# A hybrid decoder trunk: first loads in halves, another order of pairs in the in-projection, and two up-projection weights kept in place

## The chip, the cores and the metric

The kernel runs on one core of a Trainium2 chip. The metric is device time in microseconds (us) of one execution. The engines are TensorE (PE: matmuls; PEld: its weight loads), VectorE (DVE), ScalarE (ACT), GpSimd (POOL) and SyncE (SP). SP, POOL and, since this change, ACT issue DMA transfers; an issue waits in its engine's queue behind whatever stands ahead of it.

## The reference

One layer of a decoder trunk, batch 1, 1,024 positions, model width 1,024, all in float32:

```python
h = rms_norm(x, g_mix)
z = einsum("bsd,de->bse", h, w_in) + b_in          # 1024 -> 7168 columns
va, ga, xb, gb, sa, sb = split(z)                  # 1024, 1024, 1536, 1536, 1024, 1024
u = va * sigmoid(ga)
u = silu(layer_norm(causal_depthwise_conv(u, width 31)))
y_a = u @ w_a_out
v = rg_lru(causal_depthwise_conv(xb, width 4), ...)  # block-diagonal gates, linear recurrence
y_b = (v * gelu(gb)) @ w_b_out
m = sigmoid(sa) * y_a + sigmoid(sb) * y_b
x = x + m @ w_o
h = rms_norm(x, g_mlp)
x = x + square(relu(h @ w_1)) @ w_2                 # 1024 -> 4096 -> 1024
return rms_norm(x, g_final)
```

## The kernel before

**Precision.** Every float32 operand of a matmul is split into a high part, a copy rounded to the matmul's format, and a low part, the difference. Each product is three matmuls: high by high, high by low, low by high. `split` makes the low part on DVE. `split_dma` makes it by a transfer: ACT writes the negated rounded copy, a POOL DMA adds the source to it in place (256 or 512 KB), and ACT writes the high part.

**The start.** x comes twice: transposed, in tiles `xc` (two column blocks of 128 channels by 512 positions each), and in rows (`xt`), from which the squares for the RMS norm are taken. Three weight blocks, `w0` to `w2`, are loaded beside it. SP issues these loads in a fixed order: `gmix` (the norm's gain), `w0`, four `xc` tiles of the first half of the positions (half 0), `w1`, `w2`, four row tiles, the other `xc` tiles, the other row tiles. While the first data are under way, PE runs matmuls on ones (`idle_mm`). Then, with the instruction order of PE, ACT and DVE written out by hand: for each channel block `c`, ACT makes the scaled high part (`x_plain`), DVE the low part (`x_plain_low`), and PE runs `first_z`. The first half of the positions is multiplied without the row scale 1/rms. The second half needs it: `x_square` squares and sums four row tiles, `x_root(1)` makes the reciprocal root on DVE with one ACT step, `x_spread(1)` spreads it on PE into the tile `rb`, in the middle of `first_z(2, ...)`. Small DVE steps for the recurrence's decay constants (`decay`, run some at a time by `decay_on`) fill DVE's free time.

**The in-projection.** The first part goes block by block of 128 output columns (`chunk_mm`) and makes all the recurrent columns (XB) and most convolution columns (VA, GA). The second part (lines 743 and on) takes the remaining columns in pairs of blocks with seven products instead of eight (Winograd's form of Strassen's scheme). `ZPAIRS` lists the pairs: six of the Gelu gate GB, one of VA with GA, four of SA, four of SB. `zseq` interleaves the seven products of neighbouring pairs:

```python
for i in range(2, NZ):
    zseq += [(i, 1), (i, 7), (i - 1, 4), (i, 6), (i, 2), (i - 1, 3), (i, 5)]
```

In step n of `zseq` the kernel evacuates step n - 1 or n - 2 (`z_post`, `z_post2`), multiplies (`z_mm`), splits the weights for step n + 4 (`z_lhs`, of which five in seven use `split_dma`) and makes the sums for step n + 5 (`z_sums`). A pair's four outputs come out after its products 2, 5, 3 and 4. `z_out` applies Gelu to GB columns, multiplies them by the recurrence's result `h`, which SP loads some steps ahead (`z_h`), and stores the product; it applies a sigmoid to SA and SB columns and stores that. DVE also works through the 31 taps of the wide convolution here, where it has time. `ZL` gives the steps at which a pair's raw weights are loaded.

**Up-projection.** The MLP's up part is again a seven-product scheme on 16 pairs of blocks of `w_1`. `raws[i, m]` holds the raw weights of pair i, half m (512 KB each). The products 1 and 2 of the first four pairs are made early, at the end of the list `gseq`, from `raws[i, 0]` (`g_lhs` with "u"). For pairs 2 and 3 `g_lhs` drops `raws[i, 0]` after product 2. Later, in the loop over `useq`, both halves of a pair that isn't there are loaded:

```python
up_load(i, [m_ for m_ in (0, 1) if (i, m_) not in raws])
```

`GX[u0 + n]` lists extra work that is issued with step n of the early products. SP's queue there holds the row tiles of x1 that are written out (`x1d`), the loads, and the stores of the early products' results (`fd`). The split weights of this part (`gu`, `o`) get their low parts by `split_dma`.

Of the kernel before, what the change touches and what calls it, by code (L numbers as in the profile page):

```python
# [9 lines left out]
F32 = mybir.dt.float32  # L10
F32R = mybir.dt.float32r
I32 = mybir.dt.int32
AF = mybir.ActivationFunctionType
ALU = mybir.AluOpType

P = 128
# [14 lines left out]
def trunk_kernel(ctx: ExitStack, tc: tile.TileContext, x, xt_in, xt_eo, vecs, w_in, w_a_out, w_b_pl, w_b_sq,  # L31
                 w_rg, w_o, w_1, w_2, g_final, out):

    nc = tc.nc
# [9 lines left out]
    def T(name, dt=F32, shape=(P, S)):  # L44
        return tp.tile(list(shape), dt, tag="T", name=name)

    def PS(name, tag="ps"):
        return pp.tile([P, S], F32, tag=tag, name=name, bufs=1 if tag == "ps2" else 3)
# [5 lines left out]
    HALVES = (slice(0, HS), slice(HS, S))  # L54


    def load_w(w, name):

        raw = wp.tile(list(w.shape), F32, tag="raw", name=name + "_raw")
        nc.sync.dma_start(raw, w)  # L60
        return raw
# [56 lines left out]
    wp = stage.enter_context(tc.tile_pool(name="weights", bufs=2))  # L118
# [8 lines left out]
    vec = cp.tile([P, 448], F32, name="vec")  # L127

    gmix = cp.tile([P, 16], F32, name="gmix")
    nc.sync.dma_start(gmix[:, 0:8], vecs[:, 0:8])  # L130
    nc.gpsimd.dma_start(vec, vecs)
    gmix_c = gmix[:, 0:8]
    bin_c = vec[:, 8:64]
# [11 lines left out]
    xt, xc, raw0 = [], [], []  # L145
# [6 lines left out]
    def load_xc(hf, c2):  # L152
        a = T(f"xc{hf}{c2}")
        nc.sync.dma_start(a, xt_in[hf, c2])
        xc.append(a)

    def load_w0(i):
        if i < 2:
            raw0.append(load_w(w_in[(16, 0, 8)[i]], f"w{i}"))
        else:  # L160
            raw0.append(T(f"w{i}_raw").rearrange("p (k c) -> p k c", c=P))
            nc.sync.dma_start(raw0[i], w_in[(16, 0, 8)[i]])

    load_w0(0)
    for c2 in range(4):
        load_xc(0, c2)
    load_w0(1)
    load_w0(2)
# [12 lines left out]
    def xpart(a, hf, c):  # L181
        return a[hf][c // 2][:, HALVES[c % 2]]

    rs_x = {}

    def x_square(t, eng):

        hf, i = divmod(t, 4)
        if hf not in rs_x:
            rs_x[hf] = cp.tile([P, 5, 4], F32, tag="st4", name=f"stx{hf}", bufs=2)  # L190
        a, ss = xt[(t + 4) % 8], rs_x[hf][:, 0, i:i + 1]
        if eng is nc.vector:
            nc.vector.scalar_tensor_tensor(a, a, 1.0, a, ALU.mult, ALU.mult, accum_out=ss)
        else:
            nc.scalar.activation(a, a, AF.Square, accum_out=ss)
# [28 lines left out]
    def x_plain(c):  # L224

        u = xc[c // 2][:, HALVES[c % 2]]
        nc.scalar.activation(xpart(xh, 0, c), u, AF.Copy, scale=gmix_c[:, c:c + 1])

    def x_plain_low(c):
        u, h = xc[c // 2][:, HALVES[c % 2]], xpart(xh, 0, c)  # L230
        nc.vector.scalar_tensor_tensor(xpart(xl, 0, c), u, gmix_c[:, c:c + 1], h.bitcast(F32),
                                       ALU.mult, ALU.subtract)
# [8 lines left out]
    w0 = []  # L241

    def first_w(i, part):
        if part == "h":
            if i < 2:
                wh = wp.tile([P, 8, P], F32R, tag="wh", name=f"w{i}_h")
                wl = wp.tile([P, 8, P], F32R, tag="wl", name=f"w{i}_l")
            else:
                wh, wl = (T(f"w{i}_{n}", F32R).rearrange("p (k c) -> p k c", c=P) for n in "hl")
            w0.append((wh, wl))  # L250
            z0.append(PS(f"z{16 + i}"))
            nc.scalar.activation(wh, raw0[i], AF.Copy)
        else:
            nc.vector.tensor_tensor(w0[i][1], raw0[i], w0[i][0].bitcast(F32), ALU.subtract)

    def first_z(i, hf, k, which):
        w, a = {"hh": (0, xh), "lh": (1, xh), "hl": (0, xl)}[which]
# [72 lines left out]
    def decay_on(n=99):  # L330

        for _ in range(n):
            next(decaying, None)

    with tc.manual_schedule(engines={mybir.EngineType.Activation, mybir.EngineType.DVE,
                                     mybir.EngineType.PE}):
        warm = cp.tile([P, 10], F32, name="warm")
        nc.vector.memset(warm[:, 0:2], 1.0)
        nc.scalar.activation(warm[:, 0:1], warm[:, 1:2], AF.Sqrt)

        spare = PS("spare", "ps2")

        def idle_mm(n):
            for _ in range(n):
                nc.tensor.matmul(spare[:, 0:P], ones, ones, start=True, stop=True)

        idle_mm(13)
        rb["tile"] = PS("rb", "ps2")
        first_w(0, "h")
        first_w(0, "l")  # L350
        for c in range(8):
            x_plain(c)
            x_plain_low(c)
            if c == 7:
                first_w(1, "h")
                first_w(1, "l")
            for which in ("hh", "lh", "hl"):
                first_z(0, 0, c, which)
        for k in range(8):
            first_z(1, 0, k, "hh")  # L360
            first_z(1, 0, k, "hl")
        decay_on(6)
        first_w(2, "h")
        first_w(2, "l")
        decay_on(14)
        for t in range(4, 8):
            x_square(t, nc.scalar)
        for k in range(8):
            first_z(1, 0, k, "lh")
        x_root(1)  # L370
        decay_on(5)
        for k in range(8):
            first_z(2, 0, k, "hh")
            first_z(2, 0, k, "hl")
            if k == 4:
                x_spread(1)
        for k in range(8):
            first_z(2, 0, k, "lh")

        for c in range(9):  # L380
            if c < 8:
                x_scaled(1, c)
            else:
                x_root(0)
                x_spread(0)
            if 3 <= c < 7:
                x_square(c - 3, nc.scalar)
            if c:
                for which in ("hh", "lh"):
                    first_z(0, 1, c - 1, which)  # L390
                x_low(1, c - 1)
                first_z(0, 1, c - 1, "hl")
                for i in range(1, N0):
                    first_z(i, 1, c - 1, "hh")
                    first_z(i, 1, c - 1, "hl")
        for i in range(1, N0):
            for k in range(8):
                first_z(i, 1, k, "lh")
        decay()
        nc.vector.tensor_scalar(cab2, cab_c, 2.0, None, ALU.mult)  # L400
        pairs = caw[:, 8:].rearrange("p (i o j) -> p i o j", o=2, j=8)
        nc.vector.tensor_tensor(csum, pairs[:, :, 0, :], pairs[:, :, 1, :], ALU.add)
# [24 lines left out]
    VA, GA, XB, GB, SA, SB = 0, 8, 16, 28, 40, 48  # L427
# [267 lines left out]
    def later(ready, cost, f, *a):  # L695

        todo.append((ready, len(todo), cost, f, a))
# [28 lines left out]
                                 start=n == 0, stop=n == 23)  # L726
        at("P", len(halves) * (n1 - n0) * MM)

    ZPAIRS = [GB + 2 * i for i in range(6)] + [VA + 7] + [SA + 2 * i for i in range(4)]
    ZPAIRS += [SB + 2 * i for i in range(4)]  # L730
    NZ = len(ZPAIRS)
    zraw, zs, zo, zb = {}, {}, {}, {}
    zn = [0]

    def z_load(i, kk):

        zraw[i, kk] = raw = qp.tile([P, 2, 4, P], F32, tag="p", name=f"zw{i}_{kk}", bufs=4)
        c = ZPAIRS[i]
        if c < GA:
# [47 lines left out]
    for i in range(2, NZ):  # L787
        n = zseq.index((i, 1))
# [20 lines left out]
    with tc.manual_schedule(engines=ENGINES):  # L809
        for s in range(3, NC1):  # L810
# [30 lines left out]
            c = CH[s - 1]  # L841
# [27 lines left out]
            for d in range(5):  # L869
                if s - d in EXP:  # L870
# [6 lines left out]
                    t = 3 * g + d - (2 if g < 3 else 1)  # L877
# [21 lines left out]
    wp = stage.enter_context(tc.tile_pool(name="weights2", bufs=3, reuse_waits="tile"))  # L899
# [59 lines left out]
    def z_out(i, m_, hf, src, name):  # L959
        if ZPAIRS[i] < GA:  # L960
            z_u(i, ZPAIRS[i] - VA, m_, hf, src)
            return
        ci = ZPAIRS[i] + m_
        bias = bin_c[:, ci:ci + 1]
# [58 lines left out]
    with tc.manual_schedule(engines=ENGINES):  # L1023
# [159 lines left out]
        for n in range(len(zseq) + 2):  # L1183
# [9 lines left out]
            if n + 3 < len(zseq):  # L1193
                i, p = zseq[n + 3]
# [15 lines left out]
    wp = early.enter_context(tc.tile_pool(name="weights3", bufs=7, reuse_waits="tile"))  # L1210
# [191 lines left out]
    def g_lhs(w, i, p):  # L1402
        if w == "u":
            src = raws[i, 0][:, 4 * (p - 1):4 * p, :]
            if p == 2 and i > 1:
                del raws[i, 0]
        elif p in (5, 6):
            src = gs[w, i][p - 5 and 1]
        else:
            src = graw[w, i, {1: 0, 2: 1, 3: 1, 7: 0, 4: 1}[p]][:, int(p == 4)]  # L1410
        go[w, i, p] = o = T(f"g{w}{i}_{p}", F32R).rearrange("p (x k c) -> p x k c", x=2, c=P)
        if w == "a" and p in (1, 2, 7):
            nc.scalar.activation(o[:, 0], src, AF.Copy)
            later(at("A", 0.6), 0.63, low, o[:, 1], src, o[:, 0])
        else:
            split_dma(src, o[:, 0], o[:, 1])
            at("A", 1.15)
# [238 lines left out]
    raws = {}  # L1656
# [113 lines left out]
    def g_get(n, f):  # L1770
# [32 lines left out]
        0: ((up_lhs, 0, 6), (x1_rows, 4, 5, 6, 7)),  # L1803
        1: ((x1_diag, 1),), 2: ((x1_spread, 1), (up_lhs, 1, 6)),
        3: ((x1_normed, 0, 1), (x1_normed, 1, 1), (g_t, "u", 0, 1), (g_t, "u", 1, 1)),
        4: ((g_t, "u", 0, 2), (g_t, "u", 1, 2)), 5: ((g_parts, "u", 6, 0),),
        6: ((g_parts, "u", 6, 1), (g_parts, "u", 5, 0), (up_lhs, 0, 5)),
        7: ((g_parts, "u", 5, 1), (up_lhs, 1, 5), (g_t, "u", 0, 3), (g_t, "u", 1, 3))}.items()})
    BX = {}
# [147 lines left out]
    with tc.manual_schedule(engines={mybir.EngineType.Activation, mybir.EngineType.DVE,  # L1957
                                     mybir.EngineType.PE}):
        for n in range(len(useq)):
# [4 lines left out]
            while ready < min(len(useq), n + look + 1):  # L1964
                i, p = useq[ready]
# [167 lines left out]
    with tc.manual_schedule(engines={mybir.EngineType.Activation, mybir.EngineType.DVE,  # L2133
                                     mybir.EngineType.PE}):
        for n, (g, p, kk) in enumerate(dseq[:-2]):
# [41 lines left out]
            if (g, m - 4) in XADD:  # L2177
                k = XADD[g, m - 4]
# [103 lines left out]
```

## Time and profile before

| | |
|---|---|
| Median of 3 runs | 1531.3 us (1531.1 to 1531.85) |
| Profiled execution, device time | 1531.15 us |
| Its span, first to last instruction | 1529.4 us |
| Granted PE clock | 0.999 of full speed |
| First matmul on real data | 7.17 us |
| Second part of the in-projection | about 339 to 626 us |
| Early products of the up part | about 907 to 933 us |
| Last instruction's stage: time after the last matmul | some 7 us |

Times in the profile count from the start of the span. A busy share is that of a stretch. An engine's idle time is put down to what ended it; several semaphores to the one that came last.

### The profile page before, as it was taken

How to read it: one execution, taken by the hardware profiler on the slowest of the kernel's cores; microseconds unless marked ns; L12 is line 12 of the kernel's file. 1: busy time of each engine (PE TensorE's matmuls, PEld its weight loads, DVE VectorE, ACT ScalarE, POOL GpSimd, SP SyncE). 2: the span in 40 equal slices, each digit the busy share in tenths (PEclk: the TensorE clock that was granted, in tenths of full speed). 3: DMA queues.
4: the chain of work that ended last, by engine and by line, in shares of the span. 5: the costliest groups of instructions: out<-in, count | busy, mean ns of one | idle time of the engine just before them, and what ended most of it. 6: DMA issues, size and time to landing. Idle time of an engine off the chain costs nothing.

```text
span 1529.4 us, 18963 instructions
## 1 busy us (share of the span) xinstructions
PE 1519.5 (99%) x6722; PEld 1251.2 (82%) x6722; DVE 1200.0 (78%) x1636; ACT 928.3 (61%) x1299; POOL 192.3 (13%) x228
## 2 busy tenths in 40 slices
PE   9999999999999999999999999999999999999998
PEld 7878887888888888888888887888888888888886
DVE  6899996998999997788869879755555387777777
ACT  6748688576566667645575777554444455545475
POOL 0111011022222222000022332000000000101010
PEclk9999999999999999999999999999999999999999
DMA  9766779797997889964879897333333974776465
GB/s 352 188 146 154 184 159 204 196 258 209 265 261 173 186 207 271 297 226 119 269 201 302 188 205 195 138 122 111 111 111 111 302 265 131 177 211 169 107 123 153
DMA packets 130799, 296.53 MB, mean 194 GB/s; under 512 B 12896, under 2 KB 34912, under 8 KB 130704
## 3 DMA queue, kind: packets, MB, share of 16 engines
q1 hardware_dynamic: 98960, 215.92, 42.0%
q0 software_dynamic: 31600, 79.15, 28.1%
q8 instruction: 52, 0.85, 0.2%
q14 instruction: 43, 0.35, 0.1%
q10 hardware_dynamic: 144, 0.26, 0.0%
HBM read 149.79 MB, written 60.82 MB: 138 GB/s over the span
## 4 chain that ended last, share of the span: by engine, by line
PE 96%; issue 2%; DVE 1%; POOL 1%; DMA 0%; ACT 0%; POOLq 0%; ACTq 0%
PE z L725 16%; PE z L258 2%; PE d1b L2002 2%; PE d2b L2002 2%; PE d0b L2002 2%; PE d3b L2002 2%; PE d0e L2002 1%; PE d3e L2002 1%; PE d3a L2002 1%; PE d2e L2002 1%; PE d2a L2002 1%; PE d1e L2002 1%; PE d1a L2002 1%; PE d0a L2002 1%; PE rg L532 1%
## 5 line engine op out<-in xcount | busy, mean ns | idle before, releaser
L725 PE MATMUL z<-xh,win_h 128*128 128x512 f32 x368 | 115.4, 391 | 0.0
L725 PE MATMUL z<-xl,win_h 128*128 128x512 f32 x368 | 114.9, 390 | 0.0
L637 DVE SCALAR_TENSOR_TENSOR y<-u,vec,y 128x511 f32<-128x511 f32 (+14 forms) x120 | 88.2, 735 | 0.0
L725 PE MATMUL z<-xh,win_l 128*128 128x512 f32 x368 | 87.4, 389 | 0.0
L637 DVE SCALAR_TENSOR_TENSOR yt<-u,vec,yt 128x511 f32<-128x511 f32 (+6 forms) x112 | 82.5, 736 | 0.0
L637 DVE SCALAR_TENSOR_TENSOR y<-yt,csum,y 128x511 f32<-128x511 f32 (+6 forms) x112 | 82.4, 736 | 0.0
L725 PEld LDWEIGHTS z<-xh,win_h 128*128 128x128 f32 x368 | 69.1, 188 | 16.0 <-ACT win_h L67 0.5
L725 PEld LDWEIGHTS z<-xl,win_h 128*128 128x128 f32 x368 | 69.1, 188 | 14.9
L725 PEld LDWEIGHTS z<-xh,win_l 128*128 128x128 f32 x368 | 69.1, 188 | 14.6
L542 ACT ACTIVATE g<-rg,vec 96x1024 f32<-96x1024 f32 x32 | 35.5, 1110 | 72.9 <-PE rg L534 72.8
L1697 ACT ACTIVATE o<-s 128x512 fp32r<-128x512 f32 x56 | 33.7, 623 | 45.7 <-DVE s L1681 26.4
L66 POOL DMA_DIRECT2D zo<-zw x45 | 39.2, 871 | 133.8 <-ACT zo L65 110.4
L483 DVE SCALAR_TENSOR_TENSOR v<-xb,vec,v 128x1023 f32<-128x1023 f32 (+2 forms) x36 | 46.2, 1282 | 6.3 <-ACT v L474 5.3
L66 POOL DMA_DIRECT2D db_10l<-br x4 | 3.5, 877 | 339.6 <-DMA br<-in_w_dram 254.4
L66 POOL DMA_DIRECT2D win_l<-win_raw x23 | 20.0, 868 | 194.0 <-ACT win_l L65 155.9
L65 ACT ACTIVATE zo<-zw 128x512 fp32r<-128x512 f32 x45 | 28.2, 626 | 24.3 <-PE z10f L929 2.1
L1219 DVE TENSOR_TENSOR o<-s,o 128x512 fp32r<-128x512 f32 x56 | 37.2, 683 | 1.3 <-ACT o L1697 1.3
L66 POOL DMA_DIRECT2D zo<-zs x30 | 26.4, 879 | 75.9 <-ACT zo L65 63.8
L67 ACT ACTIVATE zo<-zw 128x512 fp32r<-128x512 f32 x45 | 27.9, 621 | 0.0
L578 DVE TENSOR_TENSOR_SCAN g<-a,g 128x1024 f32<-128x1024 f32 x12 | 27.5, 2291 | 0.4
L66 POOL DMA_DIRECT2D ga<-gsa x8 | 7.0, 874 | 161.0 <-DMA m<-mbd 150.8
L1219 DVE TENSOR_TENSOR o<-w_raw,o 128x512 fp32r<-128x512 f32 x38 | 25.9, 683 | 0.0
(3182 smaller groups left out, 4912.0 us busy)
## 6 DMA issues: line engine op xcount, KB each, us to landing
w_raw<-in_w_dram SPq DMA_DIRECT2D x34, 512.0 KB, 5.7
br<-in_w_dram SPq DMA_DIRECT2D x32, 512.0 KB, 6.1
ar<-fd SPq DMA_DIRECT2D x32, 512.0 KB, 7.0
zw<-in_w_in_dram SPq DMA_DIRECT2D x28, 512.0 KB, 6.9
win_raw<-in_w_in_dram SPq DMA_DIRECT2D x23, 512.0 KB, 5.0
win_l<-win_raw POOLq DMA_DIRECT2D x23, 512.0 KB, 5.2
zo<-zw POOLq DMA_DIRECT2D x45, 256.0 KB, 5.7
gates<-zg SPq DMA_DIRECT2D x32, 256.0 KB, 4.1
```

Source lines behind the costliest of these rows:

```text
L65: nc.scalar.activation(l, src, AF.Copy, scale=-1.0)
L66: nc.gpsimd.dma_start(l, src, accum_op=ALU.add)
L67: nc.scalar.activation(h, src, AF.Copy)
L258: nc.tensor.matmul(z0[i][:, HALVES[hf]], w0[i][w][:, k, :], xpart(a, hf, k), start=k == 0 and which == "hh", stop=k == 7 and which == ("hl ...
L483: nc.vector.scalar_tensor_tensor(v[:, d:S], a[:, 0:S - d], cbw_c[:, w * 12 + t:w * 12 + t + 1], v[:, d:S], ALU.mult, ALU.add)
L542: nc.scalar.activation(a, gps.pop((n, gi))[:HD, :], AF.Sigmoid, bias=(ba_c, bx_c)[gi][:, n:n + 1])
L578: nc.vector.tensor_tensor_scan(i, a, i, 0.0, ALU.mult, ALU.add)
L637: nc.vector.scalar_tensor_tensor(o[:, k:], a[:, 0:HS - k], c, o[:, k:], ALU.mult, add)
L725: nc.tensor.matmul(zps[s][:, HALVES[hf]], w[:, k, :], xw[k][part][hf], start=n == 0, stop=n == 23)
L1219: tt(l, src, h.bitcast(F32), ALU.subtract)
L1697: nc.scalar.activation(o[:, 0], src, AF.Copy)
L2002: nc.tensor.matmul(o, a, b, start=start and n == 0, stop=stop and n == len(todo) - 1, skip_group_check=not start or not stop)
```

## The change

1. At the start, `w0` and the first `xc` tile are loaded in halves, on two queues: SP takes the first half of `w0`, `gmix`, and the second half of `xc`; ACT the first half of `xc` and the second half of `w0`. `w0` is split in halves too (`first_half`), the second after channel block 2. Nine `idle_mm` instead of thirteen (each is a pair of passes in the profile).
2. Of the four squares of the row tiles 4 to 7 one (t == 6) is made by DVE, and the four stand ahead of `decay_on(14)` instead of behind it.
3. `ZPAIRS` alternates GB pairs with SA pairs; VA + 7 and the four SB pairs keep their places.
4. `raws[2, 0]` and `raws[3, 0]` are kept, and the other halves of these pairs are loaded at step u0 + 4.

```diff
-    nc.sync.dma_start(gmix[:, 0:8], vecs[:, 0:8])
     nc.gpsimd.dma_start(vec, vecs)
...
-    load_w0(0)
-    for c2 in range(4):
+    raw0.append(wp.tile([P, 8, P], F32, tag="raw", name="w0_raw"))
+    xc.append(T("xc00"))
+    nc.sync.dma_start(raw0[0][:, 0:4], w_in[16, :, 0:4])
+    nc.scalar.dma_start(xc[0][:, HALVES[0]], xt_in[0, 0, :, HALVES[0]])
+    nc.sync.dma_start(gmix[:, 0:8], vecs[:, 0:8])
+    nc.scalar.dma_start(raw0[0][:, 4:8], w_in[16, :, 4:8])
+    nc.sync.dma_start(xc[0][:, HALVES[1]], xt_in[0, 0, :, HALVES[1]])
+    for c2 in range(1, 4):
         load_xc(0, c2)
...
-            nc.scalar.activation(wh, raw0[i], AF.Copy)
+            if i:
+                nc.scalar.activation(wh, raw0[i], AF.Copy)
...
+    def first_half(n):
+        k = slice(4 * n, 4 * n + 4)
+        h, l = (a[:, k] for a in w0[0])
+        nc.scalar.activation(h, raw0[0][:, k], AF.Copy)
+        nc.vector.tensor_tensor(l, raw0[0][:, k], h.bitcast(F32), ALU.subtract)
...
-        idle_mm(13)
+        idle_mm(9)
         rb["tile"] = PS("rb", "ps2")
         first_w(0, "h")
-        first_w(0, "l")
+        first_half(0)
         for c in range(8):
             x_plain(c)
             x_plain_low(c)
+            if c == 2:
+                first_half(1)
...
         first_w(2, "h")
         first_w(2, "l")
+        for t in range(4, 8):
+            x_square(t, t == 6)
         decay_on(14)
-        for t in range(4, 8):
-            x_square(t, nc.scalar)
...
-    ZPAIRS = [GB + 2 * i for i in range(6)] + [VA + 7] + [SA + 2 * i for i in range(4)]
-    ZPAIRS += [SB + 2 * i for i in range(4)]
+    ZPAIRS = [GB, GB + 2, SA, GB + 4, SA + 2, GB + 6, VA + 7, SA + 4, GB + 8, SA + 6, GB + 10] + [SB + 2 * i for i in range(4)]
...
             src = raws[i, 0][:, 4 * (p - 1):4 * p, :]
-            if p == 2 and i > 1:
-                del raws[i, 0]
...
-        4: ((g_t, "u", 0, 2), (g_t, "u", 1, 2)), 5: ((g_parts, "u", 6, 0),),
+        4: ((up_load, 2, (1,)), (up_load, 3, (1,)), (g_t, "u", 0, 2), (g_t, "u", 1, 2)), 5: ((g_parts, "u", 6, 0),),
```

More of the change, by code (lines that the diff above doesn't have):

```diff
@@ L184, in trunk_kernel, with x_square @@
     rs_x = {}
-    def x_square(t, eng):
+    def x_square(t, dve=False):
         hf, i = divmod(t, 4)
@@ L191, in x_square @@
         a, ss = xt[(t + 4) % 8], rs_x[hf][:, 0, i:i + 1]
-        if eng is nc.vector:
+        if dve:
             nc.vector.scalar_tensor_tensor(a, a, 1.0, a, ALU.mult, ALU.mult, accum_out=ss)
@@ L386, in trunk_kernel @@
             if 3 <= c < 7:
-                x_square(c - 3, nc.scalar)
+                x_square(c - 3)
             if c:
```

## The prediction

> **What bounds the kernel now.** I read the page's engine table and chain first, then busy time by stretches, then TensorE's (PE) waits, and last the timelines of the three places that the change touches.
>
> ```profile
> span 1529.4 us, 18963 instructions
> PE 1519.5 (99%) x6722; PEld 1251.2 (82%) x6722; DVE 1200.0 (78%) x1636; ACT 928.3 (61%) x1299; POOL 192.3 (13%) x228
> PE 96%; issue 2%; DVE 1%; POOL 1%; DMA 0%; ACT 0%; POOLq 0%; ACTq 0%
> ```
> ```profile
> 340.00:538.00 198.00, 198.00 (x875) 163.99 (x874) 183.88 (x285) 127.64 (x218) 46.47 (x53) 1.00 0.86 217
> 373.00:563.00 190.00, 190.00 (x840) 157.35 (x839) 177.59 (x278) 120.54 (x208) 47.35 (x54) 1.00 0.88 221
> 933.00:945.00 12.00, 11.67 (x52) 9.34 (x50) 10.93 (x12) 11.82 (x20) 5.25 (x6) 1.00 0.82 189
> ```
> ```profile
> PE f0d L1709 <- DMA o<-s: 0.8, 1, 0.8
> ```
>
> PE is busy 99% of the span and carries 96% of the chain. In the in-projection's second part (340 to 538 us) it has no idle time at all: a new order of pairs can win nothing there, it can only lose. After the start, PE's list of waits has one entry, 0.8 us for an `o<-s` transfer in the stretch 933 to 945. So the change has two places to win in: the start, and that wait. No multiplication is added or removed.
>
> **The start.** The timeline there, by engine:
>
> ```profile
> 0.74 0.39 SPq L130 DMA_DIRECT2D gmix<-in_vecs_dram  x1
> 1.18 0.42 SPq L60 DMA_DIRECT2D w_raw<-in_w_in_dram  x1
> 1.60 5.92 PE L345 MATMUL spare<-ones 128*128 128x128 f32 x26 [1.60 <-POOL ones L113]
> 4.95 1.06 ACT L252 ACTIVATE w_h<-w_raw 128x1024 fp32r<-128x1024 f32 x1 [2.72 <-DMA w_raw<-in_w_in_dram]
> 7.17 0.70 PE L258 MATMUL z<-xh,w_h 128*128 128x512 f32 x1
> 14.51 1.06 ACT L195 ACTIVATE x<-x 128x1024 f32<-128x1024 f32 x1 [0.21 <-DMA x<-in_x_dram]
> 17.09 1.06 ACT L195 ACTIVATE x<-x 128x1024 f32<-128x1024 f32 x1 [0.15 <-DMA x<-in_x_dram]
> 18.36 1.06 ACT L195 ACTIVATE x<-x 128x1024 f32<-128x1024 f32 x1
> 16.31 0.17 DVE L286 SCALAR_TENSOR_TENSOR sm<-sm 128x12 f32<-128x12 f32 x1
> 18.80 0.17 DVE L293 TENSOR_TENSOR sm<-sm 128x12 f32<-128x12 f32 x1
> 19.54 0.17 DVE L202 TENSOR_SCALAR stx<-stx 128x4 f32<-128x4 f32 x1 [0.58 <-ACT x L195]
> 21.50 1.13 PE L217 MATMUL rb<-rd,ones 128*128 128x128 f32 x8
> ```
> ```profile
> L483 DVE SCALAR_TENSOR_TENSOR v<-xb,vec,v 128x1023 f32<-128x1023 f32 (+2 forms) x36 | 46.2, 1282 | 6.3 <-ACT v L474 5.3
> ```
>
> The loads are one stream. ACT's squares at 14.51 and 17.09 each wait for a 512 KB tile that has just landed: two tiles in 2.58 us, 1.29 each. Halves change the order within the stream, not its rate. They move its beginning: the first weight was issued at 1.18 behind gmix, and the half now goes at 0.74, so 0.44 earlier. From 1.18 to the landing that starts ACT at 4.95 are 3.77 us for one tile, 2.48 over the steady 1.29; a second issuing queue could win back part of that ramp. I bound the stream's shift by 0 (2 KB pieces may be slower) and 1.4, and take 0.5, close to the row of the issue. ACT's two issues, by SP's rows 0.39 to 0.42 each, end long before its first data.
>
> PE may begin earlier: nine pairs of warming matmuls instead of thirteen take 4 x 5.92/13 = 1.8 us less, and halves split after half a tile. That is cover only as long as nothing later holds PE back. One thing does: PE must have the row scale `rb` in the middle of the third column block. In the trace it comes at 21.50, right behind PE's arrival, and its chain is the fourth x tile: square at 18.36, `x_root` on VectorE (DVE) at 19.54, `rb` 1.96 later.
>
> Here the change moves work onto that chain. The square of the third tile (t == 6) goes to DVE, and the fourteen decay steps, which ran from 16.31 to 18.97 beside the wait, now stand behind it in DVE's queue and ahead of `x_root`. The tile lands at 17.09 - 0.5 = 16.6. No trace row shows a DVE square with a sum; the nearest, 1,023 elements of the same operation, takes 1.28 (below: ACT's 1.06; above: half as much again for the sum). So 16.6 + 1.28 + 2.66 + 1.96 = 22.5 for `rb` against 21.50. ACT's chain, a square shorter, is done earlier and no longer counts. PE waits, and everything behind it shifts: **+1.0**. With the stream's bounds +0.1 to +1.5. What PE won before 21 us is lost in this wait.
>
> **The order of pairs.** Gate pairs (GB, Gelu) and sigmoid pairs (SA, VA) now alternate. Loads, sums, splits and matmuls per pair are the same; what changes is which function ACT needs next. From the timeline of ACT at the one such border in the trace, with the transfer that follows it:
>
> ```profile
> 462.14 1.28 ACT L944 ACT_TABLE_LOAD   x1
> 463.44 0.69 ACT L944 ACTIVATE u<-z6a,vec 128x512 f32<-128x512 f32 x1
> 464.02 0.62 ACT L65 ACTIVATE zo<-zw 128x512 fp32r<-128x512 f32 x1
> 465.18 1.28 ACT L969 ACT_TABLE_LOAD   x1
> 467.06 0.62 ACT L65 ACTIVATE zo<-zs 128x512 fp32r<-128x512 f32 x1
> 480.57 1.28 ACT L980 ACT_TABLE_LOAD   x1
> ```
> ```profile
> 467.98 0.87 POOL L66 DMA_DIRECT2D zo<-zs  x1 [2.16 <-ACT zo L65]
> ```
> ```profile
> DMA to landing us min/median/max: 7.4/7.4/7.4
> DMA to landing us min/median/max: 4.2/6.7/9.3
> ```
> ```profile
> 476.19 2.72 PE z7b L929 x12
> ```
>
> Two neighbouring pairs interleave their outputs (old, new, old, new), so a border of unlike functions costs three table loads: 462.14, 465.18, 480.57. Before there was one border inside the list; now there are nine (1|2, 2|3, 3|4, 4|5, 5|6, 7|8, 8|9, 9|10, 10|11): 8 x 3 = 24 more loads of 1.30 us (462.14 to 463.44), 31 us of ACT. ACT is busy 120.5 of the 190 us from 373 to 563, so 31 fit into its 69 idle us on the whole.
>
> Locally less so. Two loads fall into neighbouring steps, ahead of ACT's `zo` splits, whose low half a DMA then finishes. The split at 467.06 is one of those delayed; its DMA was issued at 467.98 and landed after 7.4 us, at 475.4. The step that uses it, z7b, stands at 476.19 and needs it with its third matmul, 0.45 later: 1.2 to spare. With the slowest landing of this stretch (first number pair: this one DMA; second: all of 373 to 545), 9.3 instead of 7.4, PE would wait 0.7. Of the 32 splits under the eight new borders I take two that meet such a landing: **+1.4**; ends 0 (as at the border shown) and +5.6 (one at every border).
>
> The Trainium skill, page "ScalarE: Activation LUTs", section "What ACT_TABLE_LOAD costs", puts a switch to another set at about 2.66 us, load and drain together, and its rules ask to do all of one set before switching. The row does not bear out the drain (the next activation starts 1.30 after the load); by the page's price the 24 would be 64 us, nearly all of ACT's idle time here.
>
> **Up weights kept.** Two reloads of 512 KB (the first halves of pairs 2 and 3) go; the two loads that remain are issued at the fifth step of the up part instead of behind the fourth store of `f`. The pieces of timeline, POOL, SP and PE:
>
> ```profile
> 917.24 0.95 POOL L66 DMA_DIRECT2D gu<-w_raw  x1 [5.90 <-ACT gu L65]
> 937.92 0.87 POOL L66 DMA_DIRECT2D o<-s  x1 [0.65 <-ACT o L65]
> 912.63 4.68 SPq L1585 DMA_DIRECT2D x1d<-x1r  x4
> 938.81 6.63 SPq L1664 DMA_DIRECT2D w_raw<-in_w_dram  x3
> 925.32 0.72 PE L1427 MATMUL gu1a<-gu2h,gu 128*128 128x512 f32 x2
> 945.45 0.73 PE L1709 MATMUL f0d<-gu7h,o 128*128 128x512 f32 x2 [0.77 <-DMA o<-s]
> ```
> ```profile
> DMA to landing us min/median/max: 8.0/8.0/8.0
> ```
>
> The `o<-s` of 937.92, for which PE waits until 945.45, shares the engines with the three `w_raw` loads that SP issues from 938.81. With those gone it lands before its step: -0.8, and some 0.2 of slow matmuls beside it. But from 912.63 SP writes four 512 KB rows out, and `gu<-w_raw` of 917.24 needed 8.0 us (the row above) and landed at 925.25, just when PE uses it (925.32). The two kept loads now queue on SP right behind those rows: 2 x 1.29 = 2.6 us of transfers where there is no slack. They may find no free buffer so early and come later; then SP's four stores of `f` stand behind them, which nobody reads before the down-projection. Ends -1.0 and +1.6; I take half a microsecond lost of the gain: **-0.5**.
>
> **Sum.** +1.0 + 1.4 - 0.5 = +1.9. The profiled execution took 1531.15 (span 1529.4 and 1.75 around it), 0.15 under the median of the runs, 1531.3. So 1533.0. A measurement of this kernel tells about 0.2%, 3.06 us, from no change: under 1528.2 is faster, over 1534.4 slower.
>
> **Rivals.**
> *The start wins.* If the stream comes 1.4 earlier and the DVE chain is not what ends last, `rb` can't come more than the stream's 1.4 earlier than now; with the whole -1.0 of the up weights and no cost in the pairs that is 1528.7, with the 0.5 of the issue row 1529.6. Against it: the decay steps' place in DVE's queue. Chance 0.17.
> *ACT late among the alternating pairs.* A pair's seven steps take 7 x 2.72 = 19.0 us, of which ACT works 19 x 120.5/190 = 12.1; three loads make 16.0. It decides once the lead of the splits is used up: about 1.2 us at a border, as worked out above, so from landings of 8.6 us on, or from a switch that holds ACT for more than (19.0 - 12.1)/3 = 2.3 us. The first, at four of five borders, is 0.7 x 6 = 4.2 over the start's +1.0 and the -0.5: 1535.9. The second would be (12.1 + 3 x 2.66 - 19.0) x 8 = 8.6 us, but the row's 1.30 speaks against it. Chance 0.23. The page named above stands with the second: by its price ACT falls behind in every pair; that part I give 0.03.
> *The kept loads collide.* +1.6 in place of -0.5: 1535.1. For it: the landing without slack at 925; against: buffers may come free later. Chance 0.10.
> The forecast keeps 0.50.
>
> **Numbers.** The forecast's own cases lie between 1531 and 1534.3. The range 1530.0 to 1535.8 leaves out the best start (about 0.08) and the worst ACT cases (about 0.1). Slower by over 0.2%: most of the second and third rivals and a little of the forecast, 0.28. Faster by over 0.2% needs the stream's full bound and every other gain: 0.05. The rest, 0.67, is no change.
>
> **What would show it.** Right: the first `z` matmul near 5.7 us, yet a PE wait of about a microsecond before `rb`, with DVE's decay steps between the t == 6 square and `x_root`; 28 table loads in place of 4 between 340 and 626 us, ACT some 31 us busier, and a few PE waits under 1 us for `zo` transfers; no wait at f0d, perhaps one at gu1a. Wrong: `rb` before 21.3; no PE wait at all among the pairs, or many; a gain or loss of PE elsewhere than in these three places.

## The result, and the profile after

The kernel after takes 1535.05 us (median of 9 runs, 1533.4 to 1536.41), the one before 1531.11 beside it (9 runs, 1530.6 to 1531.85): a ratio of 1.0026, with a 95% interval of 1.0017 to 1.0035. It is slower by 0.26%, 3.9 us, just above the 0.2% from which the prediction calls a difference a change. The profiled execution took 1535.94, 0.9 above the median, with a span of 1534.2, 4.8 us more than the 1529.4 of before; the terms read from it below are together that 0.9 above those of the median. The page of the profile after, span, engines and chain:

```profile
span 1534.2 us, 18973 instructions
PE 1520.0 (99%) x6714; PEld 1249.4 (81%) x6714; DVE 1202.0 (78%) x1639; ACT 956.8 (62%) x1322; POOL 192.2 (13%) x228
PE 93%; DMA 3%; DVE 1%; issue 1%; ACT 0%; POOL 0%; SPq 0%; POOLq 0%; DVEq 0%; ACTq 0%
```

PE has as much work as before (1520.0 us busy against 1519.5), ACT 28.5 us more, and DMA has 3% of the chain where it had none. PE's waits after (engine, tile and line, what it waited for: us in total, times, longest):

```profile
PE spare L357 <- POOL ones L113: 1.6, 1, 1.6
PE z L270 <- ACT xh L232: 1.3, 1, 1.3
PE z4e L942 <- DMA zo<-zs: 1.2, 1, 1.2
PE gu1a L1438 <- DMA gu<-w_raw: 1.1, 1, 1.1
PE rb L222 <- DVE rd L213: 0.8, 1, 0.8
PE z7f L942 <- DMA zo<-zw: 0.5, 1, 0.5
PE z L270 <- DVE xl L236: 0.2, 1, 0.2
```

The wait at f0d is gone. Each of the three places has new ones: at the start (`z` twice, `rb`), two among the pairs (`z4e`, `z7f`), one in the up part (`gu1a`). PE waits nowhere else, but for the first warming matmul, as before.

**The start.** The timeline after; the rows of before stand in the prediction:

```profile
5.82 0.52 PE L270 MATMUL z<-xh,w_h 128*128 128x512 f32 x1
9.36 0.50 PE L270 MATMUL z<-xh,w_h 128*128 128x512 f32 x1 [1.31 <-ACT xh L232]
17.54 1.23 DVE L198 SCALAR_TENSOR_TENSOR x<-x 128x1024 f32<-128x1024 f32 x1 [0.28 <-DMA x<-in_x_dram]
18.69 0.17 DVE L298 SCALAR_TENSOR_TENSOR sm<-sm 128x12 f32<-128x12 f32 x1
21.27 0.16 DVE L207 TENSOR_SCALAR stx<-stx 128x4 f32<-128x4 f32 x1
18.82 1.06 ACT L200 ACTIVATE x<-x 128x1024 f32<-128x1024 f32 x1 [1.41 <-DMA x<-in_x_dram]
21.47 0.20 ACT L97 ACTIVATE stx<-stx 128x4 f32<-128x4 f32 x1 [1.50 <-DVE stx L207]
23.22 1.13 PE L222 MATMUL rb<-rd,ones 128*128 128x128 f32 x8 [0.79 <-DVE rd L213]
```

PE begins 1.35 us earlier (5.82 against 7.17) and is at `rb` 1.72 later (23.22 against 21.50). From 17.54 to 21.27 DVE does the third tile's square and then the fourteen decay steps, while ACT, done with the fourth tile, waits 1.50 us for DVE's first step of `x_root`. And the row tiles come later than before, not earlier: the fourth starts ACT at 18.82 instead of 18.36.

**The pairs.** The groups of ACT's table loads between 340 and 630 us after, the stretch 373 to 563 by engine, and the timeline ahead of the wait at z4e:

```profile
L982 ACT ACT_TABLE_LOAD x14 | 18.0, 1283 | 2.8 <-PE z5a L942 0.5 <-PE z10a L942 0.5 <-PE z8a L942 0.5
L993 ACT ACT_TABLE_LOAD x13 | 16.7, 1283 | 0.2
L957 ACT ACT_TABLE_LOAD x1 | 1.3, 1283 | 0.0
```
```profile
373.00:563.00 190.00, 188.32 (x829) 155.32 (x829) 175.94 (x275) 145.11 (x226) 46.31 (x53) 1.00 0.87 218
```
```profile
427.12 1.28 ACT L993 ACT_TABLE_LOAD   x1
430.16 1.28 ACT L982 ACT_TABLE_LOAD   x1
435.21 1.28 ACT L993 ACT_TABLE_LOAD   x1
437.18 0.62 ACT L65 ACTIVATE zo<-zs 128x512 fp32r<-128x512 f32 x1
438.39 0.87 POOL L66 DMA_DIRECT2D zo<-zs  x1 [1.98 <-ACT zo L67]
446.96 0.72 PE L942 MATMUL z4e<-xh,zo 128*128 128x512 f32 x2 [1.21 <-DMA zo<-zs]
```

28 loads, and idle time of PE where it had none: 1.68 us. Three table loads stand in the 10 us ahead of the split at 437.18; its transfer, issued at 438.39, landed after 8.5 us, and PE had been waiting for it since 445.75.

**The up part.** The timeline after:

```profile
916.62 4.63 SPq L1596 DMA_DIRECT2D x1d<-x1r  x4
921.43 2.71 SPq L1675 DMA_DIRECT2D w_raw<-in_w_dram  x2
921.24 0.95 POOL L66 DMA_DIRECT2D gu<-w_raw  x1 [5.90 <-ACT gu L65]
930.50 0.74 PE L1438 MATMUL gu1a<-gu2h,gu 128*128 128x512 f32 x2 [1.10 <-DMA gu<-w_raw]
```

SP issues the two kept pairs' loads right behind the four rows of x1, within 0.2 us of the `gu` transfer of which PE has no slack. That lands after 9.2 us (8.0 before), and PE waits.

By the trace that is +1.72 at the start, +2.2 among the pairs (two waits, with the slow matmul behind each) and +0.87 in the up part (+2.1 at gu1a to gu3a, less 0.2 that was lost there before and 1.05 at f0d): together the 4.8 of the span.

### The profile page after: what moved, and what is told of

Same layout as the page of the kernel before. It is cut to its first block, busy times and chain, and to the rows that moved or that the text cites. A ratio compares the mean times of both kernels' runs of the same rounds, so it can differ in the third digit from the quotient of the medians.

```text
span 1534.2 us, 18973 instructions
## 1 busy us (share of the span) xinstructions
PE 1520.0 (99%) x6714; PEld 1249.4 (81%) x6714; DVE 1202.0 (78%) x1639; ACT 956.8 (62%) x1322; POOL 192.2 (13%) x228
## 4 chain that ended last, share of the span: by engine, by line
PE 93%; DMA 3%; DVE 1%; issue 1%; ACT 0%; POOL 0%; SPq 0%; POOLq 0%; DVEq 0%; ACTq 0%
PE z L739 16%; PE d1b L2013 2%; PE d2b L2013 2%; PE d0b L2013 2%; PE d3b L2013 2%; PE d0e L2013 1%; PE d3e L2013 1%; PE d3a L2013 1%; PE d2e L2013 1%; PE d2a L2013 1%; PE d1e L2013 1%; PE d1a L2013 1%; PE d0a L2013 1%; PE z L270 1%; PE rg L546 1%
## 5 line engine op out<-in xcount | busy, mean ns | idle before, releaser
L497 DVE SCALAR_TENSOR_TENSOR v<-xb,vec,v 128x1023 f32<-128x1023 f32 (+2 forms) x36 | 46.2, 1283 | 5.8 <-ACT v L488 4.8
```

Source lines behind the costliest of these rows:

```text
L497: nc.vector.scalar_tensor_tensor(v[:, d:S], a[:, 0:S - d], cbw_c[:, w * 12 + t:w * 12 + t + 1], v[:, d:S], ALU.mult, ALU.add)
```

## The experiments

Twelve kernels, each in 11 runs beside runs of the kernel before on the same chip. What lies around the span scatters from 1.7 to 3.7 us, so the median of the spans is shown too; it is the sharper of the two. By the time alone, e1 (only just) to e3 are slower and e10 to e12 faster than the kernel before; the intervals of e4 to e9 include no change, and what is said of these rests on their spans and traces.

| run | time, median us | ratio to before, interval | span, median us | before's span | difference |
|---|---|---|---|---|---|
| e1 start | 1532.67 | 1.0009 (1.0000 to 1.0018) | 1530.9 | 1529.3 | +1.6 |
| e2 order | 1532.84 | 1.0011 (1.0002 to 1.0020) | 1531.1 | 1529.3 | +1.8 |
| e3 keep | 1533.30 | 1.0012 (1.0003 to 1.0021) | 1531.1 | 1529.3 | +1.8 |
| e4 order, one function | 1531.39 | 1.0002 (0.9993 to 1.0011) | 1529.4 | 1529.3 | +0.1 |
| e5 halves | 1531.94 | 1.0003 (0.9994 to 1.0012) | 1530.2 | 1529.4 | +0.8 |
| e6 VectorE's order | 1532.70 | 1.0007 (0.9999 to 1.0016) | 1530.5 | 1529.4 | +1.1 |
| e7 keep, not early | 1530.28 | 0.9993 (0.9984 to 1.0002) | 1528.2 | 1529.4 | -1.2 |
| e8 switches, old order | 1532.31 | 1.0004 (0.9995 to 1.0013) | 1530.0 | 1529.4 | +0.6 |
| e9 loads two steps later | 1530.33 | 0.9994 (0.9985 to 1.0002) | 1528.4 | 1529.5 | -1.1 |
| e10 keep, vec late | 1529.30 | 0.9987 (0.9978 to 0.9996) | 1527.5 | 1529.5 | -2.0 |
| e11 and halves | 1529.76 | 0.9990 (0.9981 to 0.9998) | 1528.0 | 1529.5 | -1.5 |
| e12 and split earlier | 1529.70 | 0.9988 (0.9979 to 0.9997) | 1527.9 | 1529.6 | -1.7 |

**e1, e2, e3: each part alone.** The edits are the diff's own hunks on the kernel before: the start (all ahead of `ZPAIRS`), `ZPAIRS`, and the two behind it.

> Only the start of the change. Theory (VectorE's square of the third row tile and the fourteen decay steps stand ahead of x_root, and the load stream comes 0.45 us later): the row scale rb starts near 23.2 us instead of 21.5, everything behind shifts, time +1.7 us (1532.8 beside 1531.1). Rival (the three parts act on one another, so that the start alone is nearly free because a later stage catches up): +0 to +0.5 us. No PE wait at z, gu1a; the 0.8 us wait at f0d stays.

PE's wait at `rb`, in e1's list of waits:

```profile
PE rb L222 <- DVE rd L213: 0.8, 1, 0.8
```

`rb` at 23.20, so 1.7 late, and the span +1.6: as the trace had it. What the text expected of the f0d wait was not seen: it came at the next step, f1d (0.7).

> Only the alternating order of pairs. Theory: 28 table loads in place of 4 between 340 and 626 us, ACT about 28 us busier, and two or three short PE waits for zo transfers, +2.2 us in all (1533.3 beside 1531.1). Rival (the waits seen in the changed kernel came from the shift of the start against the transfers, not from the order): no wait, within 0.3 us of the kernel before. Second rival (ACT late at every border): +4 us or more.

```profile
PE z4e L928 <- DMA zo<-zs: 1.4, 1, 1.4
```

+1.8. The wait at z4e comes without the other parts too, so it belongs to the order. The one at z7f does not come again (its transfer needed 10.0 us, e2's slowest 8.7); whether it was a chance of that execution or came with the later start is not shown.

> Only the kept up weights and the early loads of their other halves. Theory: the f0d wait of 0.8 us goes (with the slow matmuls beside it about 1.05 us), but the two loads run against the low halves of gu, PE waits about 1.3 us at gu1a and 0.3 each at gu2a and gu3a: net +0.9 us (1532.0 beside 1531.1). Rival (the collision is an accident of the changed kernel's time line): -0.5 to -1.0 us (1530.1 to 1530.6).

```profile
PE gu1a L1425 <- DMA gu<-w_raw: 1.7, 1, 1.7
PE gu3a L1425 <- DMA gu<-w_raw: 0.4, 1, 0.4
```

+1.8, more than the +0.9 that was read from the changed kernel's trace; single runs scatter most of all here, between 1531.18 and 1534.63. The rival, a gain, fell. So every part loses by itself. Their sum is +5.2, the whole change +4.0 (its median span is 1533.3, against the 1529.3 beside e1 to e3): the parts add up, but for 1.2 us that the intervals (some 1.4 us each way, per kernel) don't let me assign.

**e4 and e8: the order or the table loads.** e4 is e2 with the sigmoids replaced by Gelu; e8 is the order of before with the functions of the new order:

```diff
 e4
-            nc.scalar.activation(g, src..., AF.Sigmoid, bias=bias)
+            nc.scalar.activation(g, src..., AF.Gelu_apprx_tanh, bias=bias)
 e8
+    ZF = [AF.Gelu_apprx_tanh if i in (0, 1, 3, 5, 8, 10) else AF.Sigmoid for i in range(NZ)]
...
-            nc.scalar.activation(a, src, AF.Gelu_apprx_tanh, bias=bias)
+            nc.scalar.activation(a, src, ZF[i], bias=bias)
```

> The alternating order with Gelu in place of the sigmoid in all of this part's outputs, so the computed gates differ and no border needs another table. Theory (the table loads delay the splits whose low halves PE then misses): no table load between the pairs, ACT no busier than before, no PE wait for zo, time within 0.3 us of the kernel before (1530.8 to 1531.4). Rival (the other order of loads and stores on the queues slows the low halves): the waits at z4e and z7f remain, +1.5 to +2.2 us.

The same split and transfer as above, in e4's timeline:

```profile
433.96 0.61 ACT L65 ACTIVATE zo<-zs 128x512 fp32r<-128x512 f32 x1
435.16 0.87 POOL L66 DMA_DIRECT2D zo<-zs  x1 [1.89 <-ACT zo L67]
443.94 0.61 PE L928 MATMUL z4e<-xh,zo 128*128 128x512 f32 x2
```

+0.1, no wait among the pairs, one table load. The transfer was no faster (8.4 us against 8.5), but it was issued 8.8 us ahead of the third product of its step (435.16 to 443.94); with the table loads it was 7.4 (438.39 to the 445.75 at which PE began to wait). 1.4 us of ACT's lead is what the loads took, and that is PE's wait. The new order of loads and stores costs nothing by itself that these runs show.

> The pairs in the order of before, but the functions by place in the list as in the changed order (Gelu at places 0, 1, 3, 5, 8, 10, sigmoid at the others), so the computed gates differ and the table loads are those of the changed kernel with the transfers of the kernel before. Theory (the table loads alone are enough): 28 loads, one or two PE waits for zo of 0.5 to 1.5 us, time +1 to +2 us. Rival (it takes the other order of transfers as well): within 0.3 us of the kernel before.

```profile
PE z3b L930 <- DMA zo<-zs: 1.4, 1, 1.4
PE z2f L930 <- DVE zc L462: 0.6, 1, 0.6
```

28 loads, and +0.6 in the median span, below the +1 to +2 of the theory and above the 0.3 of the rival. The two waits of the profile, one of them for DVE, are not the loads' alone: the profiled execution is the slowest of the eleven (span 1532.0, the others 1529.4 to 1531.4). ACT's timeline and the transfer for which z3b waits:

```profile
389.48 1.28 ACT L970 ACT_TABLE_LOAD   x1 [3.53 <-DMA hgd<-hb]
395.31 0.87 POOL L66 DMA_DIRECT2D zo<-zs  x1 [2.17 <-ACT zo L65]
```

In the kernel before, ACT waits 1.79 us at this place for the same store, and the transfer goes out at 390.87. Of the 4.4 us by which it is later here, two table loads are 2.6 and the late store 1.7; by these numbers next to nothing of the 1.4 us of waiting would be left with the loads alone (an estimate). So it is e2 against e4 that shows what the loads cost in the new order, and e8 says only that they may cost something without it. How much depends on which transfers they push into which landings. In the new order the border of pairs 3 and 4 (counted from 0, as in the prediction) is such a place, in the changed kernel and in e2: its three loads stand ahead of the split for z4e.

**e5 and e6: the start's two halves.** e5 takes the loads in halves, `first_half` and the nine warming matmuls alone, e6 the squares' place and the DVE square alone.

> Of the start only the loads in halves on two queues (with w0 split in halves and nine warming matmuls); the squares all on ScalarE and the decay steps ahead of them, as before. Theory (of the start's 1.72 us by the trace, the later load stream makes 0.45 and VectorE's queue 1.27): fourth row tile landed at 18.8 instead of 18.34, rb at 21.95, time +0.4 to +0.5 us. Rival (the stream's lateness does the whole, VectorE's queue none): rb after 22.9, +1.4 or more.

```profile
8.16 0.51 PE L270 MATMUL z<-xh,w_h 128*128 128x512 f32 x1 [0.74 <-ACT xh L232]
18.88 1.06 ACT L200 ACTIVATE x<-x 128x1024 f32<-128x1024 f32 x1
22.32 1.05 PE L222 MATMUL rb<-rd,ones 128*128 128x128 f32 x8
```

> Of the start only the third row tile's square on VectorE and the squares ahead of the fourteen decay steps; loads whole, as before. Theory: tile landed at 17.09, square 1.15, decays 2.67, so x_root about 20.8 and rb about 22.8 in place of 21.5: time +1.3 us. Rival (the decay steps would fit beside the wait, the stream alone is late): rb at 21.5 to 21.8, +0 to +0.3 us.

```profile
23.02 1.13 PE L217 MATMUL rb<-rd,ones 128*128 128x128 f32 x8 [1.24 <-DVE rd L208]
```

e6 is DVE's queue, as expected: +1.1, `rb` late by 1.5, of which 0.27 is that this execution's row tiles landed later (18.6). e5 lost more than the theory said: +0.8, `rb` at 22.32 instead of 21.95, and there PE does *not* wait. It came late itself, although its first product was at 5.76: it waits for the second half of the first xc tile (8.16), and its products then follow at the pace of the low parts until 11.5 us (e12, below, finds which of DVE's steps makes them late). In the whole change this loss and DVE's lie on top of each other (PE arrives at 22.43 and waits until 23.22), so e5 and e6 add to 1.9 and e1 is 1.6. The row tiles land later with halves: the fourth at 18.76 to 18.86 in the three kernels with halves seen so far, at 18.31 to 18.61 in the seven without.

**e7 and e9: where the two loads are issued.** e7 keeps the weights, with the two loads left where they were; e9 issues them at step 6, two later than e3 and the change.

```diff
 e7
-            if p == 2 and i > 1:
-                del raws[i, 0]
 e9, beside it
-        6: ((g_parts, "u", 6, 1), ...
+        6: ((up_load, 2, (1,)), (up_load, 3, (1,)), (g_parts, "u", 6, 1), ...
```

> The two raw weights are kept (two loads fewer), but the other two are loaded where they were before, behind the fourth store of f. Theory (the loss comes from where the two loads are issued, not from keeping): no wait at gu1a to gu3a beyond the 0.2 us of before, f0d's wait shorter or gone, -0.3 to -0.9 us (1530.3 to 1530.9). Rival (keeping the two buffers takes them from others, whose loads then wait): slower by 0.5 us or more, with PE waits elsewhere than at gu1a.

> The kept up weights with the early loads of their other halves two steps later than in the change (sixth step instead of the fourth; issued near 928 to 934 us, when the low halves of gu have landed at about 929.6). Theory (the loss is the two loads' meeting with the low halves of gu): no PE wait at gu1a to gu3a beyond 0.5 us, none at f0d, time 0.8 to 1.2 us below the kernel before. Rival (any load ahead of the four stores of f costs): +0.5 us or more.

The `gu<-w_raw` transfers issued between 915 and 925 us (KB each, median us to landing), in the kernel before, in e3 and in e7:

```profile
gu<-w_raw POOLq DMA_DIRECT2D x3, 256.0 KB, 6.7
```
```profile
gu<-w_raw POOLq DMA_DIRECT2D x3, 256.0 KB, 9.9
```
```profile
gu<-w_raw POOLq DMA_DIRECT2D x3, 256.0 KB, 7.2
```

And where SP issues the two loads, in e3 and in e9:

```profile
917.57 3.27 SPq L1662 DMA_DIRECT2D w_raw<-in_w_dram  x2
```
```profile
930.93 1.25 SPq L1662 DMA_DIRECT2D w_raw<-in_w_dram  x2
```

Two loads of 512 KB among them stretch the median landing by 3 us; taken away from there, it is nearly as before. Two steps later in the list is 13 us later on SP's queue, behind two of the stores of `f`, when the last of the three `gu` transfers (issued at 922.39, 6.3 us to landing) has landed. Both kernels gain 1.1 to 1.2 us. In their profiles e7 waits 0.5 us at gu1a, more than the 0.2 expected, and nowhere at f0d; e9 waits at neither for a transfer, but 0.4 us at f0d for DVE. It is the place of the loads that cost, by two steps.

**e10 to e12: what feeds the start.** The theory by then: the start is set by the bytes ahead of the fourth row tile. On e7's kernel `vec` goes behind the row tiles; e11 adds the halves, e12 moves the second split:

```diff
 e10
-    nc.gpsimd.dma_start(vec, vecs)
...
     for t in range(4, 8):
         load_x(t)
+    nc.sync.dma_start(vec, vecs)
...
-        decay_on(6)
...
-        decay_on(14)
...
-        decay_on(5)
...
+            if s == 4:
+                decay_on(25)
 e12, on e11
-            if c == 2:
+            if c == 1:
                 first_half(1)
```

> The kept up weights without early loads (1.1 us faster alone), and at the start whole loads in the order of before, but vec (229 KB, by the stream's 1.28 us for 524 KB some 0.56 us of it) behind the four row tiles instead of ahead of the second xc tile; the decay steps, which read vec, run later, in blocks 4 and 5 of the first part. Theory (the start is set by the bytes that stand ahead of the fourth row tile): second xc tile near 7.6 us instead of 8.1, fourth row tile near 17.85, rb near 20.95, so another 0.5 us: 1.6 us below the kernel before (1529.6 beside 1531.2). Rival (ScalarE's and VectorE's steps per block, not the stream, feed PE): rb stays at 21.4 to 21.5, no more than the 1.1 us. Second rival (the delayed decay steps hold VectorE up): PE waits of 0.5 us or more between 80 and 130 us.

```profile
PE 99%; DMA 0%; DVE 0%; issue 0%; ACT 0%; SPq 0%
17.79 1.06 ACT L195 ACTIVATE x<-x 128x1024 f32<-128x1024 f32 x1
20.92 1.13 PE L217 MATMUL rb<-rd,ones 128*128 128x128 f32 x8
```

As worked out: `rb` at 20.92, -2.0 in span, a ratio of 0.9987 (0.9978 to 0.9996). The 0.58 us at `rb` is the tile's: from the square of the fourth row tile to `rb` are 3.13 us here and 3.14 before (18.36 to 21.50), so taking the decay steps away added nothing. Beside e7, which kept the loads of before at the start, the span is 0.8 lower, a little more than that; e7's profile had 0.5 us of waiting at gu1a that is not there in e10's. PE's list of waits ends with the start, and 99% of the chain is PE. It is faster than the kernel before, and has the lowest median of the fourteen.

> As the run before, with the first loads in halves on two queues, w0 split in halves and nine warming matmuls added. Theory (an earlier first product is only spent waiting, and the halves bring the stream 0.4 us later): first product near 5.8 us, but rb 0.3 to 0.8 us later than in the run before, time 0.3 to 0.8 us above it. Rival (with vec out of the way PE is fed from the early start on): rb and time 0.3 us or more below it.

The timeline of e11:

```profile
9.06 0.68 DVE L266 TENSOR_TENSOR w_l<-w_raw,w_h 128x512 fp32r<-128x512 f32 x1
9.66 3.39 DVE L236 SCALAR_TENSOR_TENSOR xl<-xc,gmix,xh 128x512 fp32r<-128x512 f32 x5
21.30 1.05 PE L222 MATMUL rb<-rd,ones 128*128 128x128 f32 x8
```

> The run before with one line moved: the second half of w0 is split after channel block 1, where ScalarE and VectorE wait 0.9 us for the second xc tile, instead of after block 2, where VectorE is what feeds PE. Theory (rb came 0.38 us later with halves, 21.30 against 20.92, because this split of 0.60 us stands ahead of block 3 on VectorE): no wait of PE for the low part of block 3, rb at 20.9 to 21.0, now set by the fourth row tile (landed 17.85, chain of 3.16 behind it), time that of the kernel with whole loads within 0.2 us (1529.1 to 1529.5). Rival (the loads on two queues are what is late): rb stays at 21.3. Neither expects halves to beat whole loads, since the row tile's landing then decides.

```profile
18.01 1.06 ACT L200 ACTIVATE x<-x 128x1024 f32<-128x1024 f32 x1 [0.16 <-DMA x<-in_x_dram]
21.15 1.13 PE L222 MATMUL rb<-rd,ones 128*128 128x128 f32 x8 [0.15 <-DVE rd L213]
```

First product at 5.72 in e11, yet `rb` 0.38 later than in e10 (+0.5 in span). The split of w0's second half (9.06) stands on DVE just ahead of the low parts that PE is waiting for. With it one block earlier, in DVE's idle time (e12), PE arrives 0.3 sooner and waits for `rb`, which is now set by the fourth row tile: 18.01 to 21.15 is the 3.14 that the same chain takes in e10 (17.79 to 20.92, 3.13). So the split was the cause of e11's delay, and the rest of e12's (0.23) is the stream. The same stretch is 3.43 in e11 (17.87 to 21.30) and 3.44 in e5 (18.88 to 22.32), where the split stands at the same place, at 10.06: of the 0.82 by which e5's `rb` was late, some 0.3 is this split and 0.5 the stream. Halves win nothing in any of the five kernels that have them.

## Why the prediction was right or wrong

The time, 1535.05, lies within the range, 2.05 above the predicted 1533.0; slower by 0.26%, it is not the "no change" that I thought likeliest. The three places, the signs of two terms and the mechanism of each held. All three terms came out above their forecast, by 0.7, 0.8 and 1.4 us in the profile: all errors went the same way, and the range covered the time by its width.

**Start, +1.0, came as +1.72.** The chain on DVE was right step by step: third tile, square (1.28 taken, 1.15 to the next step), decay steps (2.66 taken, 2.58 until `x_root`), `x_root` to `rb` (1.96 taken, 1.95). The step that failed is the stream's shift: taken 0.5 earlier from the row of the issue, it was 0.45 later (the third tile started its square at 17.54; 16.6 was predicted), outside my bounds of 0 and 1.4. What of the halves delays it, the two queues or the 2 KB pieces that I named, stays open. An earlier issue is not an earlier stream: in e10 and e11, where `vec` is out of the way, the second xc tile landed at 7.50 without halves and at 7.61 with them. The Trainium skill, page "DMA: Bandwidth & Descriptors", section "Issuing engines are not separate DMA queues", says that transfers issued on several engines interleave on the same 16 and only issue time is saved; that agrees, and the 0.44 us of issue time did not come out at the other end. I also wrote that what PE won before 21 us is lost at `rb`; PE had won nothing, it was late by itself (e5), and the split of w0's second half on DVE, which I had put at nothing, was a part of it (e12).

**Pairs, +1.4, came as +2.2 in the profile, +1.8 in e2.** The counts held: 28 table loads, ACT 28.5 us busier (31 predicted), two waits (one of them 1.2 us, over the 1 that I gave them). What failed is the term "1.2 to spare" from the one border that the trace showed: at z4e the loads left a lead of 7.4 us, so that a landing of 8.5 was enough for 1.2 us of waiting, where I needed 9.3 for 0.7. (The 4.2, 6.7 and 9.3 given there for 373 to 545 us hold up to about 458; to 545 it is 3.3, 6.4 and 9.4, which moves the 0.7 by 0.1.) "ACT late among alternating pairs", at four of five borders, did not come. The Trainium skill's page "ScalarE: Activation LUTs", section "Rules for kernel authors", asks to do all of one set before switching; e4 and e2, which differ by 1.7 us in span, agree. The Trainium skill's figure for the load itself, about 1,283 ns (the same page, section "What ACT_TABLE_LOAD costs"), is what all 28 took; the drain that it adds does not show here: the next activation begins 1.30 us after the start of the load (427.12 to 428.42).

**Up weights, -0.5, came as +0.87 in the profile, +1.8 in e3.** Both mechanisms were named, and both were seen: the wait at f0d went, and the loads met the `gu` transfers without slack. The step that failed is the choice of "half a microsecond lost of the gain" between the ends -1.0 and +1.6. The doubt in it, that the loads would find no free buffer so early, was wrong: they went out right behind the rows, whose last issue ends at 921.25 in the changed kernel (loads at 921.43 and 922.9) and at 917.39 in e3 (from 917.57 on). The rival "The kept loads collide" described it, with +1.6, and should have had more than 0.10: the row on which it rested, a landing at 925.25 for a use at 925.32, was in the trace. That its 1535.1 is nearly the measured time is luck: it is reached with a start and pairs that are cheaper, and an up part that is dearer, than in the changed kernel's profile. e7 shows the gain itself at -1.2, close to the -1.0 taken.

## What to carry to other kernels

Where PE is busy 99% of the time, an edit off its path has little to win and slack to lose. So list the transfers that land just before their use, and ask of every moved load and every switch of ACT's function which of those it meets: here a load's place by two steps was worth 2.9 us (e3 against e9, whose loads went out 13 us apart). An earlier first product is no gain while the data behind it come at the same rate; what moved the start was taking the 224 KB of `vec` (229 thousand bytes), which nothing on the path needs yet, out from ahead of the tile that decides. And a chain that is free beside a wait, as the decay steps were, is not free once it stands in front of what ends the wait.

## What the runs showed of the hardware

The first loads in halves over two issuing queues brought the first half of `w0` at 4.40 to 4.62 us, where the whole tile came at 4.89 to 5.08, but the stream behind them landed 0.1 to 0.6 us later than with whole tiles, most of it where `vec` shared the engines (second xc tile 8.51 to 8.62 against 8.06 to 8.37; without `vec` ahead 7.61 and 7.75 against 7.50). What delays it in that time was not tried apart: the queues and the length of the pieces changed together. Two plain loads of 512 KB, 2.6 us of the stream by its own rate, took the three `gu` transfers beside them from 8.0, 6.7 and 6.7 us to 9.9, 9.8 and 10.9 (before and e3): each lost between 1.9 and 4.2 us. And the 0.8 us for an `o<-s` transfer that the profile of before shows at f0d is not fixed to that place: it stood at f1d in e1, e6 and e8 (0.7, 0.7, 0.5), was 0.8 at f0d in e5 and 0.2 there in e2, and did not come in e4.
